# A two-layer trunk kernel: two of four weight sums of a pair made by adding transfers, unsplit weights in a ring of blocks

## The chip, the cores and the metric
The kernel runs on one core of one Trainium2 chip. The metric is the device time of one launch, in microseconds (us), as the median of several runs. A core has five engines with queues of their own, each in order: TensorE (PE, matmuls), VectorE (DVE), ScalarE (ACT), GpSimd (POOL) and SyncE (SP, which here issues most of the DMAs). They wait for each other and for DMAs by semaphores.

## What is computed
Sixteen learned tokens are put ahead of 512 (528 positions, width 1024), which then go through four sub-layers, each followed by a LayerNorm of `alpha * x + f(x)`: a chunked gated DeltaNet (GDN), a gated ConvFFN, a short gated convolution, and a second ConvFFN. The change touches how the weights of the last three are brought in and prepared:

```python
def short_conv_mixer(h, w_in, conv_w, w_out):
    b_gate, c_gate, xv = jnp.split(h @ w_in, 3, axis=-1)
    u = causal_dwconv(c_gate * xv, conv_w)
    return (b_gate * u) @ w_out

def conv_ffn(h, w_up, conv_w, w_down):
    u, gate = jnp.split(h @ w_up, 2, axis=-1)
    u = causal_dwconv(u, conv_w)
    return (jax.nn.silu(u) * gate) @ w_down
```

All of it is float32. D_FF is 2816 (22 blocks of 128), the depthwise convolutions are three wide.

## The kernel before
Channels lie on the 128 partitions and positions run along the rows. `h` holds the activations; `hh` and `hl` are their high and low parts. A weight strip (128 output channels by up to 1024 inputs, so up to 8 blocks of 128 by 128) is loaded as float32 (`raw`), and `split` makes `wh` (ACT, L88) and `wl` (DVE, L89) of it. A block product takes three matmuls: high by high (L272), high by low (L273), low by high (L274).

**Pairs.** Most up-projections of the FFNs, and most input projections of the short conv, are done two strips at a time (18 pairs in each FFN, 8 in the short conv, 44 in all). Each strip is cut into two halves of four blocks, the positions into two halves as well, and the two by two product is done with seven half products rather than eight. Their weights are A11, A12, A22 and four sums: S1 = A21 + A22, S2 = S1 + A11, S3 = A21 + A11, S4 = S2 + A12. Each sum is one DVE add over 128x512 (L210, L212, L214, L216), and each of the seven is then split. `PREP` gives the order in which that is done.

**Staging.** A list of jobs (a pair, or one strip) holds all weights in order of use. `pump` loads the next job as soon as its raw tiles are free and prepares the next piece as soon as the ring of split weights (`wh`, `wl`: 32 blocks, and 24 more once the second part is open) has room; `get` and `product` call it each time a weight is used, so the loads and splits fall between the engine's other instructions at fixed places in the program. Unsplit weights stand in tiles of 8 blocks: two while GDN runs (first part), four afterwards; a pair takes two. The sum tile `s` has 4 blocks.

**Stages of a sub-layer.** An FFN works through its 22 blocks in groups of 4, 6, 6 and 6. The first group is the lead: its up-projections are not paired, since the sums of the activations for the pairs (`sums_a`, `sums_b`, L883) are made in the meantime. `emit` writes the convolution and silu; `gated` multiplies in the gate (L851) and splits the result into `gh`, `gl`; `down` multiplies by the down weights (`pd`) and adds to `h` (L760 for the first group, L762 after). The other groups run as `pairs`, each followed by its `down`. The short conv has a lead of two blocks (`bu0`, `bu1`), then eight pairs. The first pair's weights are loaded and split while the lead still runs, so pair work and lead work share the queues of DVE and ACT there. That is the place of the terms in the prediction.

Of the kernel before, what the change touches and what calls it, by code (L numbers as in the profile page):

```python
# [30 lines left out]
CH = 106  # L31
# [3 lines left out]
LEVELS = (1, 2, 4, 8, 16, 32, 64)  # L35
# [18 lines left out]
NCST = 3 * P  # L54
# [5 lines left out]
PREP = ("A11", "S1", "S2", "A12", "S3", "A22", "S4")  # L60


class Unit:
    def __init__(self, seg, pos, n, hi, lo):
        self.seg, self.pos, self.n, self.hi, self.lo = seg, pos, n, hi, lo


class Job:
    def __init__(self, srcs, nk):
        self.srcs, self.nk, self.raws, self.units, self.ready, self.n = srcs, nk, [], {}, False, 0  # L70


@with_exitstack
def tile_hybrid_trunk(ctx, tc, xt, par, cst, msk, w_ba, w_qkv, w_z, w_ao, w_bi, w_bo, w_up, w_dn, out):
    nc = tc.nc
    V, S, G, TE = nc.vector, nc.scalar, nc.gpsimd, nc.tensor

    cpool = ctx.enter_context(tc.tile_pool(name="cpool", bufs=1))
    hpool = ctx.enter_context(tc.tile_pool(name="hpool", bufs=1))
    wpool = ctx.enter_context(tc.tile_pool(name="wpool", bufs=1))  # L80
    lnp = ctx.enter_context(tc.tile_pool(name="lnp", bufs=1))

    h = hpool.tile([P, KD, T], F32, name="h")
    hh = hpool.tile([P, KD, T], F32R, name="hh")
# [2 lines left out]
    def split(hi, lo, src):  # L87
        S.activation(hi, src, AF.Copy)  # L88
        V.tensor_tensor(lo, src, hi.bitcast(F32), ALU.subtract)  # L89
# [5 lines left out]
    cst_sb = cpool.tile([P, NCST], F32, name="cst_sb")
    msk_sb = cpool.tile([P, len(LEVELS), CH], U8, name="msk_sb")
# [12 lines left out]
    jobs = []  # L109
# [32 lines left out]
    n_gdn = len(jobs) - 8  # L142
# [12 lines left out]
    add_ffn(1)  # L155


    SEG = (32, 24)
    segs = []
    pools = []  # L160
    HOLD6, HOLD8 = 7, 5
    FFN_GRP, SC_GRP = (4, 2), (4, 2)
    STAG = 2
    OUTS = {1: 0, 3: 2, 5: 4, 6: 6, 7: 7}

    def open_part(pool):
        x = len(segs)
        segs.append((pool.tile([P, SEG[x], P], F32R, name=f"wh{x}"), pool.tile([P, SEG[x], P], F32R, name=f"wl{x}")))
        pools.append(pool)

    open_part(wpool)
    state = {"use": 0, "load": 0, "prep": 0, "raws": 0, "base": 0, "held": 0, "seg": 0, "pos": 0, "pairs": 0}
    live = []

    def room(n):

        g_, p_ = state["seg"], state["pos"]
        if p_ + n > SEG[g_]:
            g_, p_ = (g_ + 1) % len(segs), 0
        for u in live:  # L180
            if u.seg == g_ and u.pos < p_ + n and p_ < u.pos + u.n:
                return None
        state["seg"], state["pos"] = g_, p_ + n
        u = Unit(g_, p_, n, segs[g_][0][:, p_ : p_ + n, :], segs[g_][1][:, p_ : p_ + n, :])
        live.append(u)
        return u

    def done(u):
        live.remove(u)

    def load(job):
        for i, src in enumerate(job.srcs):
            x = (state["raws"] - state["base"]) % (2 * len(pools)) // 2
            x = 1 - x if len(pools) == 2 else x
            nm = f"raw{state['raws']}"
# [4 lines left out]
            job.raws.append(raw)  # L200
            state["raws"] += 1
        state["held"] += len(job.srcs)

    def sums(job, what):

        a, b = job.raws
        a11, a12, a21, a22 = a[:, 0:4, :], a[:, 4:8, :], b[:, 0:4, :], b[:, 4:8, :]
        if what == "S1":
            job.s = pools[-1].tile([P, 4, P], F32, name=f"s{job.n}", tag="s", bufs=1)
            V.tensor_tensor(job.s, a21, a22, ALU.add)  # L210
        elif what == "S2":
            V.tensor_tensor(job.s, job.s, a11, ALU.add)  # L212
        elif what == "S3":
            V.tensor_tensor(a21, a21, a11, ALU.add)  # L214
        elif what == "S4":
            V.tensor_tensor(job.s, job.s, a12, ALU.add)  # L216
        own = {"A11": a11, "A12": a12, "A22": a22, "S3": a21}
        return own[what] if what in own else job.s

    def prep_step(job):  # L220

        pair = len(job.srcs) == 2
        what = PREP[len(job.units)] if pair else "all"
        u = room(4 if pair else job.nk)
        if u is None:
            return False
        job.units[what] = u
        if pair:
            split(u.hi, u.lo, sums(job, what))
        else:  # L230
            step = job.nk if job.n else 4
            for k in range(0, job.nk, step):
                split(u.hi[:, k : k + step, :], u.lo[:, k : k + step, :], job.raws[0][:, k : k + step, :])
        job.ready = len(job.units) == (len(PREP) if pair else 1)
        return True

    def pump(end=None):
        while True:
            i = state["load"]
            if i < len(jobs) and i < (n_gdn + 4 if len(pools) == 1 else len(jobs)) \  # L240
                    and state["held"] + len(jobs[i].srcs) <= 2 * len(pools):
                jobs[i].n = i
                load(jobs[i])
                state["load"] += 1
                continue
            i = state["prep"]
            if i >= state["load"] or (end is not None and i >= end):
                return
            if not prep_step(jobs[i]):
                return  # L250
            if jobs[i].ready:
                state["prep"] += 1
                state["held"] -= len(jobs[i].srcs)
# [12 lines left out]

    def mm_steps(ps, u, nk, xh, xl, k0, c0, n, start=True, stop=True, every=2, **kw):
        hi, lo = (u.hi, u.lo) if isinstance(u, Unit) else u
        for k in range(nk):
            r_h = xh[:, k0 + k, c0 : c0 + n]  # L270
            r_l = xl[:, k0 + k, c0 : c0 + n]
            TE.matmul(ps, hi[:, k, :], r_h, start=start and k == 0, stop=False, **kw)  # L272
            TE.matmul(ps, hi[:, k, :], r_l, start=False, stop=False, **kw)  # L273
            TE.matmul(ps, lo[:, k, :], r_h, start=False, stop=stop and k == nk - 1, **kw)  # L274
# [398 lines left out]
    state["base"] = state["raws"]  # L673
# [446 lines left out]
```

## Time and profile before
| what | us |
|---|---|
| median of 3 runs | 1340.49 |
| lowest, highest | 1340.34, 1340.72 |
| time of the profiled execution | 1339.88 |
| its span in the profile | 1338.1 |
| first LayerNorm begins (after GDN) | 413.0 |
| second begins (after the first FFN) | 771.4 |
| third begins (after the short conv) | 954.2 |
| last matmul of the last LayerNorm's means | 1324.2 |

The span runs from the first to the last instruction; the time of an execution adds what lies around it (1.8 us here). In the profile a line such as L89 is the line of the kernel; groups carry the busy time, the mean of one instruction, and the idle time of the engine ahead of it with what ended it. The granted clock of PE is a share of full speed; over the whole span it was 0.996.

### The profile page before, as it was taken

What the parts mean: (1) busy time and instruction counts of PE and PEld (TensorE: products, weight loads), DVE (VectorE), ACT (ScalarE), POOL (GpSimd) and SP (SyncE); (2) the same over time, 40 slices, a digit from 0 to 9 for tenths busy, and PEclk for the clock granted to TensorE, in tenths of its full rate; (3) what the DMA queues carried; (4) which work ended last, traced back from release to release, by engine and by line L of the source; (5) the groups of instructions that cost most, each with busy time, mean ns of one, the idle gap of its engine ahead of it and who ended that gap; (6) DMA issues with size and microseconds to landing.
All of it is one profiled execution on the core that took longest, in us unless ns stands there. A gap on an engine that the chain in (4) does not pass through costs nothing.

```text
span 1338.1 us, 26463 instructions
## 1 busy us (share of the span) xinstructions
PE 1297.5 (97%) x10673; PEld 1251.8 (94%) x10673; DVE 1059.5 (79%) x1934; ACT 766.2 (57%) x1621; POOL 92.0 (7%) x132
## 2 busy tenths in 40 slices
PE   7999999999999999999999999899999999999996
PEld 6899989999899999999999999899998998998996
DVE  6667676776567998969869789899699896886976
ACT  5676767776454646636537465466365573663644
POOL 0322333311110000000000000000000000000000
PEclk9999999999999999999999999899999999999999
DMA  5211111111161142522522412324124342242221
GB/s 199 64 48 33 49 48 35 46 48 33 48 222 45 43 150 67 155 64 87 151 64 84 138 56 79 104 95 150 41 64 126 95 142 79 78 144 72 82 70 64
DMA packets 38395, 115.85 MB, mean 87 GB/s; under 512 B 4224, under 2 KB 7808, under 8 KB 38272
## 3 DMA queue, kind: packets, MB, share of 16 engines
q1 hardware_dynamic: 37632, 112.04, 27.1%
q0 software_dynamic: 640, 2.12, 0.5%
q8 instruction: 83, 1.36, 0.4%
q14 instruction: 40, 0.33, 0.1%
HBM read 112.05 MB, written 2.10 MB: 85 GB/s over the span
## 4 chain that ended last, share of the span: by engine, by line
PE 74%; DVE 16%; ACT 4%; issue 2%; DMA 2%; POOL 2%; SPq 0%; ACTq 0%; POOLq 0%; DVEq 0%
PE pd L273 8%; PE pd L274 8%; PE pd L272 8%; PE px L272 6%; PE px L274 6%; PE px L273 6%; DVE wl L89 3%; PE pz L272 3%; PE pz L273 3%; PE pz L274 3%; PE ps L274 2%; PE ps L273 2%; PE ps L272 2%; PE pq L272 1%; PE pq L274 1%
## 5 line engine op out<-in xcount | busy, mean ns | idle before, releaser
L88 ACT ACTIVATE wh<-raw 128x512 fp32r<-128x512 f32 (+3 forms) x321 | 238.3, 746 | 199.5 <-PE pd L273 82.5
L89 DVE TENSOR_TENSOR wl<-raw,wh 128x512 fp32r<-128x512 f32 (+3 forms) x321 | 264.9, 835 | 63.4 <-ACT wh L88 62.8
L272 PE MATMUL pd<-gh,wh 128*128 128x256 f32 (+3 forms) x704 | 213.2, 306 | 4.8 <-DVE bu L851 3.9
L273 PE MATMUL pd<-gl,wh 128*128 128x256 f32 (+3 forms) x704 | 214.3, 305 | 1.1 <-DVE gl L89 1.0
L274 PE MATMUL pd<-gh,wl 128*128 128x256 f32 (+3 forms) x704 | 213.3, 303 | 0.0
L272 PEld LDWEIGHTS pd<-gh,wh 128*128 128x128 f32 x704 | 132.6, 190 | 11.1 <-DVE bu L851 4.1
L273 PEld LDWEIGHTS pd<-gl,wh 128*128 128x128 f32 x704 | 133.8, 190 | 7.9 <-DVE gl L89 2.1
L274 PEld LDWEIGHTS pd<-gh,wl 128*128 128x128 f32 x704 | 133.7, 190 | 5.8
L88 ACT ACTIVATE wh<-s 128x512 fp32r<-128x512 f32 x132 | 83.2, 630 | 85.0 <-PE pd L273 34.7
L272 PE MATMUL ps<-hh,wh 128*128 128x264 f32 x384 | 114.7, 300 | 0.9 <-ACT acc L411 0.9
L274 PE MATMUL ps<-hh,wl 128*128 128x264 f32 x384 | 115.1, 300 | 0.0
L273 PE MATMUL ps<-hl,wh 128*128 128x264 f32 x384 | 114.3, 298 | 0.0
L273 PE MATMUL pu<-hl,wh 128*128 128x258 f32 (+3 forms) x368 | 105.5, 290 | 0.0
L272 PE MATMUL pu<-hh,wh 128*128 128x258 f32 (+3 forms) x368 | 104.2, 288 | 0.7 <-ACT hh L739 0.7
L274 PE MATMUL pu<-hh,wl 128*128 128x258 f32 (+3 forms) x368 | 104.6, 288 | 0.3 <-DVE wl L89 0.3
L89 DVE TENSOR_TENSOR wl<-s,wh 128x512 fp32r<-128x512 f32 x132 | 90.7, 687 | 15.0 <-ACT wh L88 12.0
L272 PE MATMUL px<-hh,wh 128*128 128x258 f32 (+1 forms) x352 | 99.5, 283 | 0.5 <-ACT sc L933 0.5
L274 PE MATMUL px<-sumh,wl 128*128 128x258 f32 (+1 forms) x352 | 99.7, 283 | 0.0
L273 PE MATMUL px<-suml,wh 128*128 128x258 f32 (+1 forms) x352 | 99.5, 283 | 0.0
L272 PE MATMUL px<-sumh,wh 128*128 128x258 f32 (+1 forms) x352 | 99.4, 282 | 0.0
L274 PE MATMUL px<-hh,wl 128*128 128x258 f32 (+1 forms) x352 | 99.1, 282 | 0.0
L273 PE MATMUL px<-hl,wh 128*128 128x258 f32 (+1 forms) x352 | 99.1, 282 | 0.0
(296 smaller groups left out, 3807.4 us busy)
## 6 DMA issues: line engine op xcount, KB each, us to landing
raw<-in_w_up_dram SPq DMA_DIRECT2D x88, 512.0 KB, 3.8
raw<-in_w_dn_dram SPq DMA_DIRECT2D x48, 384.0 KB, 3.5
raw<-in_w_bi_dram SPq DMA_DIRECT2D x24, 512.0 KB, 4.1
raw<-in_w_qkv_dram SPq DMA_DIRECT2D x23, 512.0 KB, 3.7
raw<-in_w_z_dram SPq DMA_DIRECT2D x8, 512.0 KB, 3.7
raw<-in_w_ao_dram SPq DMA_DIRECT2D x8, 512.0 KB, 3.6
raw<-in_w_dn_dram SPq DMA_DIRECT2D x16, 256.0 KB, 2.7
raw<-in_w_bo_dram SPq DMA_DIRECT2D x8, 384.0 KB, 3.7
```

Of the source, the lines that this page charges most:

```text
L88: S.activation(hi, src, AF.Copy)
L89: V.tensor_tensor(lo, src, hi.bitcast(F32), ALU.subtract)
L272: TE.matmul(ps, hi[:, k, :], r_h, start=start and k == 0, stop=False, **kw)
L273: TE.matmul(ps, hi[:, k, :], r_l, start=False, stop=False, **kw)
L274: TE.matmul(ps, lo[:, k, :], r_h, start=False, stop=stop and k == nk - 1, **kw)
```

## The change
A pair's weights are no longer loaded as two strips of 8 blocks. Five pieces of 4 blocks (256 KB) are loaded by SP, in the order `LOAD`: A21 as the base of S1, A21 again as the base of S3, A11, A12, A22. POOL then issues an accumulating DMA onto each of the first two: A22 onto S1, A11 onto S3. S2 and S4 stay DVE adds (now L241, written onto S1's place). So a pair reads 28 blocks from HBM where it read 16.

Unsplit weights now stand in a ring of blocks, 16 in the first part and 24 more in the second; each piece takes the next free place, and the places of a job are given back when the whole job has been split. `pump` loads piece by piece. To make room, the constants and masks that only GDN uses move to a pool that is given back after it. At three starts of a down stage the high by high matmuls of all streams come ahead of their low parts.

```diff
+LOAD = ("S1", "S3", "A11", "A12", "A22")
...
+class Ring:
+    def room(self, n):
+        g_, p_ = self.at
+        if p_ + n > self.sizes[g_]:
+            g_, p_ = (g_ + 1) % len(self.parts), 0
+        if any(u.seg == g_ and u.pos < p_ + n and p_ < u.pos + u.n for u in self.live):
+            return None
...
-    SEG = (32, 24)
+    WSEG, RSEG = (32, 24), (16, 24)
+    wring, rring = Ring(WSEG), Ring(RSEG)
...
-            raw = pools[x].tile([P, KD, P], F32, name=nm, tag="raw", bufs=2)
-            step = job.nk if state["raws"] else 4
-            for k in range(0, job.nk, step):
-                nc.sync.dma_start(raw[:, k : k + step, :], src[:, k : k + step, :])
...
-        if what == "S1":
-            job.s = pools[-1].tile([P, 4, P], F32, name=f"s{job.n}", tag="s", bufs=1)
-            V.tensor_tensor(job.s, a21, a22, ALU.add)
-        elif what == "S2":
-            V.tensor_tensor(job.s, job.s, a11, ALU.add)
-        elif what == "S3":
-            V.tensor_tensor(a21, a21, a11, ALU.add)
-        elif what == "S4":
-            V.tensor_tensor(job.s, job.s, a12, ALU.add)
...
+    def load_step(job):
+        pair = len(job.srcs) == 2
+        what = LOAD[len(job.raws)] if pair else "all"
+        u = rring.room(4 if pair else job.nk)
+        if u is None:
+            return False
+        raw = u.aps[0]
+        job.raws[what] = u
+        if pair:
+            a, b = job.srcs
+            part = {"A11": a[:, 0:4], "A12": a[:, 4:8], "A21": b[:, 0:4], "A22": b[:, 4:8]}
+            first, *more = {"S1": ("A21", "A22"), "S3": ("A21", "A11")}.get(what, (what,))
+            nc.sync.dma_start(raw, part[first])
+            for x in more:
+                nc.gpsimd.dma_start(raw, part[x], accum_op=ALU.add)
...
+            raw = job.raws["S1" if what in ("S2", "S4") else what].aps[0]
+            more = {"S2": "A11", "S4": "A12"}.get(what)
+            if more:
+                V.tensor_tensor(raw, raw, job.raws[more].aps[0], ALU.add)
+            split(hi, lo, raw)
...
+        if job.ready:
+            for r in job.raws.values():
+                rring.done(r)
```

Rows of an engine's queue follow, in program order. A row has the line, the operation, what it writes and reads (a number in a name only tells tiles apart; `raw0`, `raw1` are the two parts of the ring), its shape, and the semaphores it waits for: DMAHW for DMAs of SP, DMASW for those of POOL, and the engines.

DVE in the lead of the short conv, before. `raw132` and `raw133` are the two strips of the first pair, `raw134` is the second pair's; `bu1` is the second block of the lead:

```order
L851 TENSOR_TENSOR bu1_10218<-bu1_10218,pu106_7_0_10397 128x258 [waits PE_49]
L89 TENSOR_TENSOR hl_69<-sc_5027,hh_68 128x2x258 [waits Activation_49]
L89 TENSOR_TENSOR wl0_83<-raw132_10306,wh0_82 128x512 [waits DMAHW2_49,Activation_49]
L89 TENSOR_TENSOR wl0_83<-raw132_10306,wh0_82 128x512 [waits Activation_49]
L210 TENSOR_TENSOR s114_10320<-raw133_10308 128x512 [waits DMAHW3_49]
L89 TENSOR_TENSOR wl0_83<-raw133_10308,wh0_82 128x512 [waits Activation_49]
L214 TENSOR_TENSOR raw133_10308<-raw133_10308,raw132_10306 128x512 [waits DVE_49]
L89 TENSOR_TENSOR wl0_83<-s114_10320,wh0_82 128x512 [waits Activation_49]
L89 TENSOR_TENSOR wl1_5016<-raw134_10314,wh1_5015 128x512 [waits DMAHW4_49,Activation_49]
L212 TENSOR_TENSOR s114_10320<-s114_10320,raw132_10306 128x512 [waits DVE_49]
L89 TENSOR_TENSOR wl0_83<-raw133_10308,wh0_82 128x512 [waits Activation_49]
L851 TENSOR_TENSOR bu1_10218<-bu1_10218,pu106_7_1_10422 128x256 [waits PE_49]
```

DVE at that place now; `raw1_4982` holds A21's sums for the first pair, then the second pair's pieces:

```order
L241 TENSOR_TENSOR raw1_4982<-raw1_4982,raw0_87 128x512 [waits DVE_49]
L119 TENSOR_TENSOR wl0_86<-raw1_4982,wh0_85 128x512 [waits DMASW5_49]
L119 TENSOR_TENSOR wl0_86<-raw0_87,wh0_85 128x512 [waits DMAHW4_49,Activation_49]
L119 TENSOR_TENSOR wl0_86<-raw1_4982,wh0_85 128x512 [waits Activation_49]
L861 TENSOR_TENSOR bu0_10122<-bu0_10122,pu105_6_0_10243 128x258 [waits PE_49]
L861 TENSOR_TENSOR bu0_10122<-bu0_10122,pu105_6_1_10268 128x256 [waits PE_49]
L241 TENSOR_TENSOR raw1_4982<-raw1_4982,raw0_87 128x512 [waits DVE_49]
L119 TENSOR_TENSOR wl1_4981<-raw1_4982,wh1_4980 128x512 [waits DMAHW7_49]
L119 TENSOR_TENSOR gl_4990<-bu0_10122,gh_4989 128x514 [waits Activation_49]
L119 TENSOR_TENSOR wl1_4981<-raw1_4982,wh1_4980 128x512 [waits Activation_49]
L861 TENSOR_TENSOR bu1_10140<-bu1_10140,pu106_7_0_10309 128x258 [waits PE_49]
L861 TENSOR_TENSOR bu1_10140<-bu1_10140,pu106_7_1_10334 128x256 [waits PE_49]
```

Before, both gates of `bu0` came ahead of the pair and the second gate of `bu1` stood behind seven steps of it. Now the first pair's work down to S2's split stands ahead of both gates of `bu0`, and S4's add with splits between them and the two gates of `bu1`; L210 and L214 are gone.

ACT at that place now (`bc2` is the start of a third block's product, `gh` the high part of a gated block, `hh` that of an activation sum):

```order
L1022 ACTIVATE bc2_10001<-pu104_4_1_10144 128x258 [waits PE_49]
L118 ACTIVATE wh0_85<-raw0_87 128x512 [waits DMAHW4_49,PE_49]
L118 ACTIVATE wh1_4980<-raw1_4982 128x512 [waits DMAHW7_49,PE_49,Activation_49]
L118 ACTIVATE wh0_85<-raw1_4982 128x512 [waits DVE_49]
L118 ACTIVATE wh1_4980<-raw0_87 128x512 [waits DMASW6_49,PE_49,Activation_49]
L118 ACTIVATE gh_4989<-bu0_10122 128x514 [waits DVE_49]
L118 ACTIVATE wh1_4980<-raw1_4982 128x512 [waits DVE_49]
L118 ACTIVATE gh_4989<-bu1_10140 128x514 [waits DVE_49]
```

Row by row: `gh` of `bu0` stands behind a split that waits for POOL's DMA of the second pair (DMASW6). Before, `gh` of `bu0` was issued ahead of the pair's splits and `gh` of `bu1` behind four of them.

DVE in the lead of the first FFN, before (`c1_2` and `c1_3` are the last two blocks of the lead, `raw52` to `raw55` strips of down weights, `raw56` and `raw57` the first pair):

```order
L89 TENSOR_TENSOR wl1_5016<-raw53_6037,wh1_5015 128x512 [waits DMAHW3_49,Activation_49]
L851 TENSOR_TENSOR c1_2_5952<-c1_2_5952,pu47_6_1_6094 128x258 [waits PE_49]
L89 TENSOR_TENSOR wl1_5016<-raw54_6041,wh1_5015 128x512 [waits DMAHW4_49,Activation_49]
L851 TENSOR_TENSOR c1_3_5964<-c1_3_5964,pu48_7_0_6128 128x258 [waits PE_49]
L89 TENSOR_TENSOR gl_5024<-c1_2_5952,gh_5023 128x516 [waits Activation_49]
L89 TENSOR_TENSOR wl1_5016<-raw55_6045,wh1_5015 128x512 [waits DMAHW5_49,Activation_49]
L851 TENSOR_TENSOR c1_3_5964<-c1_3_5964,pu48_7_1_6153 128x258 [waits PE_49]
L883 SCALAR_TENSOR_TENSOR sc_5027<-sc_5027,h_67 128x520
L89 TENSOR_TENSOR wl1_5016<-raw56_6051,wh1_5015 128x512 [waits DMAHW6_49,Activation_49]
L89 TENSOR_TENSOR wl0_83<-raw56_6051,wh0_82 128x512 [waits Activation_49]
L210 TENSOR_TENSOR s56_6065<-raw57_6053 128x512 [waits DMAHW7_49]
L89 TENSOR_TENSOR gl_5024<-c1_3_5964,gh_5023 128x516 [waits Activation_49]
```

DVE there now:

```order
L119 TENSOR_TENSOR wl1_4981<-raw1_4982,wh1_4980 128x512 [waits DMAHW4_49]
L119 TENSOR_TENSOR wl1_4981<-raw1_4982,wh1_4980 128x512 [waits DMAHW5_49]
L119 TENSOR_TENSOR wl1_4981<-raw1_4982,wh1_4980 128x512 [waits DMAHW6_49]
L119 TENSOR_TENSOR wl1_4981<-raw1_4982,wh1_4980 128x512 [waits DMASW0_49,Activation_49]
L861 TENSOR_TENSOR c1_2_5908<-c1_2_5908,pu47_6_0_6019 128x258 [waits PE_49]
L861 TENSOR_TENSOR c1_2_5908<-c1_2_5908,pu47_6_1_6044 128x258 [waits PE_49]
L241 TENSOR_TENSOR raw1_4982<-raw1_4982 128x512 [waits DVE_49]
L119 TENSOR_TENSOR wl0_86<-raw1_4982,wh0_85 128x512 [waits DMAHW1_49,Activation_49]
L119 TENSOR_TENSOR gl_4990<-c1_2_5908,gh_4989 128x516 [waits Activation_49]
L119 TENSOR_TENSOR wl0_86<-raw1_4982,wh0_85 128x512 [waits Activation_49]
L861 TENSOR_TENSOR c1_3_5920<-c1_3_5920,pu48_7_0_6078 128x258 [waits PE_49]
L861 TENSOR_TENSOR c1_3_5920<-c1_3_5920,pu48_7_1_6103 128x258 [waits PE_49]
```

The split of S1, which waits for POOL's DMA (DMASW0), and S2's add and split have moved ahead of the gates of `c1_3`; before, two splits and the add of S1 stood between those gates and `gl`.

More of the change, by code (lines that the diff above doesn't have):

```diff
@@ L60, with __init__, done @@
 PREP = ("A11", "S1", "S2", "A12", "S3", "A22", "S4")
+LOAD = ("S1", "S3", "A11", "A12", "A22")
 class Unit:
-    def __init__(self, seg, pos, n, hi, lo):
-        self.seg, self.pos, self.n, self.hi, self.lo = seg, pos, n, hi, lo
+    def __init__(self, seg, pos, n, aps):
+        self.seg, self.pos, self.n, self.aps = seg, pos, n, aps
+class Ring:
+    def __init__(self, sizes):
+        self.sizes, self.parts, self.live, self.at = sizes, [], [], (0, 0)
+    def room(self, n):
[4 more added lines that the diff above has]
+            return None
+        self.at = g_, p_ + n
+        u = Unit(g_, p_, n, [t_[:, p_ : p_ + n, :] for t_ in self.parts[g_]])
+        self.live.append(u)
+        return u
+    def done(self, u):
+        self.live.remove(u)
 class Job:
     def __init__(self, srcs, nk):
-        self.srcs, self.nk, self.raws, self.units, self.ready, self.n = srcs, nk, [], {}, False, 0
+        self.srcs, self.nk, self.n = srcs, nk, 0
+        self.raws, self.units, self.loaded, self.ready = {}, {}, False, False
 @with_exitstack
@@ L81, in tile_hybrid_trunk @@
     lnp = ctx.enter_context(tc.tile_pool(name="lnp", bufs=1))
+    gctx = ExitStack()
+    gp = gctx.enter_context(tc.tile_pool(name="gp", bufs=1))
     h = hpool.tile([P, KD, T], F32, name="h")
@@ L94, in tile_hybrid_trunk @@
     par_sb = cpool.tile([P, NPAR], F32, name="par_sb")
[L95 to L96 removed]
+    cst_sb = gp.tile([P, NCST], F32, name="cst_sb")
+    msk_sb = gp.tile([P, len(LEVELS), CH], U8, name="msk_sb")
     ba_raw = lnp.tile([P, KD, 16], F32, name="ba_raw", tag="c", bufs=CB)
@@ L166, in open_part @@
     def open_part(pool):
-        x = len(segs)
-        segs.append((pool.tile([P, SEG[x], P], F32R, name=f"wh{x}"), pool.tile([P, SEG[x], P], F32R, name=f"wl{x}")))
-        pools.append(pool)
+        x = len(rring.parts)
+        wring.parts.append((pool.tile([P, WSEG[x], P], F32R, name=f"wh{x}"), pool.tile([P, WSEG[x], P], F32R, name=f"wl{x}")))
+        rring.parts.append((pool.tile([P, RSEG[x], P], F32, name=f"raw{x}"),))
     open_part(wpool)
-    state = {"use": 0, "load": 0, "prep": 0, "raws": 0, "base": 0, "held": 0, "seg": 0, "pos": 0, "pairs": 0}
@@ L173, in tile_hybrid_trunk @@
[L173 to L195, printed above, removed]
-            raw = pools[x].tile([P, KD, P], F32, name=nm, tag="raw", bufs=2)
-            step = job.nk if state["raws"] else 4
-            for k in range(0, job.nk, step):
-                nc.sync.dma_start(raw[:, k : k + step, :], src[:, k : k + step, :])
-            job.raws.append(raw)
-            state["raws"] += 1
-        state["held"] += len(job.srcs)
@@ L204, in sums @@
-    def sums(job, what):
-        a, b = job.raws
-        a11, a12, a21, a22 = a[:, 0:4, :], a[:, 4:8, :], b[:, 0:4, :], b[:, 4:8, :]
-        if what == "S1":
-            job.s = pools[-1].tile([P, 4, P], F32, name=f"s{job.n}", tag="s", bufs=1)
-            V.tensor_tensor(job.s, a21, a22, ALU.add)
-        elif what == "S2":
-            V.tensor_tensor(job.s, job.s, a11, ALU.add)
-        elif what == "S3":
-            V.tensor_tensor(a21, a21, a11, ALU.add)
-        elif what == "S4":
-            V.tensor_tensor(job.s, job.s, a12, ALU.add)
-        own = {"A11": a11, "A12": a12, "A22": a22, "S3": a21}
-        return own[what] if what in own else job.s
+    state = {"use": 0, "load": 0, "prep": 0, "pairs": 0}
@@ new lines, in tile_hybrid_trunk @@
+    done = wring.done
+    def load_step(job):
[13 more added lines that the diff above has]
+                nc.gpsimd.dma_start(raw, part[x], accum_op=ALU.add)
+        else:
+            step = job.nk if job.n else 4
+            for k in range(0, job.nk, step):
+                nc.sync.dma_start(raw[:, k : k + step, :], job.srcs[0][:, k : k + step, :])
+        job.loaded = len(job.raws) == (len(LOAD) if pair else 1)
+        return True
@@ L223, in prep_step @@
         what = PREP[len(job.units)] if pair else "all"
-        u = room(4 if pair else job.nk)
+        u = wring.room(4 if pair else job.nk)
         if u is None:
@@ L227, in prep_step @@
         job.units[what] = u
+        hi, lo = u.aps
         if pair:
-            split(u.hi, u.lo, sums(job, what))
+            raw = job.raws["S1" if what in ("S2", "S4") else what].aps[0]
[3 more added lines that the diff above has]
+            split(hi, lo, raw)
         else:
+            raw = job.raws["all"].aps[0]
             step = job.nk if job.n else 4
             for k in range(0, job.nk, step):
-                split(u.hi[:, k : k + step, :], u.lo[:, k : k + step, :], job.raws[0][:, k : k + step, :])
+                split(hi[:, k : k + step, :], lo[:, k : k + step, :], raw[:, k : k + step, :])
         job.ready = len(job.units) == (len(PREP) if pair else 1)
+        if job.ready:
+            for r in job.raws.values():
+                rring.done(r)
         return True
@@ L239, in pump @@
             i = state["load"]
-            if i < len(jobs) and i < (n_gdn + 4 if len(pools) == 1 else len(jobs)) \
-                    and state["held"] + len(jobs[i].srcs) <= 2 * len(pools):
+            if i < len(jobs) and (len(rring.parts) == 2 or i < n_gdn + 4):
                 jobs[i].n = i
-                load(jobs[i])
-                state["load"] += 1
-                continue
+                if load_step(jobs[i]):
+                    state["load"] += jobs[i].loaded
+                    continue
             i = state["prep"]
-            if i >= state["load"] or (end is not None and i >= end):
+            if i >= state["load"] or (end is not None and i >= end) or not prep_step(jobs[i]):
                 return
[L249 to L253, printed above, removed]
+            state["prep"] += jobs[i].ready
     def get():
@@ L267, in mm_steps @@
     def mm_steps(ps, u, nk, xh, xl, k0, c0, n, start=True, stop=True, every=2, **kw):
-        hi, lo = (u.hi, u.lo) if isinstance(u, Unit) else u
+        hi, lo = u.aps if isinstance(u, Unit) else u
         for k in range(nk):
@@ L292, in tile_hybrid_trunk @@
     strict = cst_sb[:CH, C_STR : C_STR + CH]
-    strict_r = cpool.tile([P, CH], F32R, name="strict_r")
+    strict_r = gp.tile([P, CH], F32R, name="strict_r")
     V.tensor_copy(strict_r[:CH], strict)
-    one1 = cpool.tile([P, P], F32, name="one1")
+    one1 = gp.tile([P, P], F32, name="one1")
     V.memset(one1, 1.0)
@@ L310, in bcm @@
         return ap.unsqueeze(1).to_broadcast([ap.shape[0], n, ap.shape[1]])
-    with ExitStack() as gctx:
-        gp = gctx.enter_context(tc.tile_pool(name="gp", bufs=1))
+    with gctx:
         pm = gctx.enter_context(tc.tile_pool(name="pm", bufs=2, space=PSUM))
```

5 lines of the change are left out of this document (1 added, 4 removed).

## The prediction
> **What bounds the kernel now.** I read the busy shares first, then stage windows, then the waits of the matmul engine (PE), then the timeline of the places where it waited. Page, its first part and the chain that ended last:
> ```profile
> span 1338.1 us, 26463 instructions
> PE 1297.5 (97%) x10673; PEld 1251.8 (94%) x10673; DVE 1059.5 (79%) x1934; ACT 766.2 (57%) x1621; POOL 92.0 (7%) x132
> ...
> PE 74%; DVE 16%; ACT 4%; issue 2%; DMA 2%; POOL 2%; SPq 0%; ACTq 0%; POOLq 0%; DVEq 0%
> ```
> PE is busy 97% of the span. A share is an average, so here are windows over the pair stages (columns: window, length, busy us of each engine, granted clock, DMA share, GB/s):
> ```profile
> 500.00:680.00 180.00, 179.51 (x1494) 178.92 (x1493) 147.09 (x252) 96.59 (x179) 0.00 (x0) 1.00 0.34 102
> 680.00:800.00 120.00, 119.99 (x996) 119.51 (x995) 99.40 (x192) 66.61 (x125) 0.00 (x0) 1.00 0.30 90
> 870.00:960.00 90.00, 90.00 (x749) 89.71 (x748) 76.57 (x140) 46.62 (x89) 0.00 (x0) 1.00 0.31 100
> 1030.00:1150.00 120.00, 120.00 (x830) 111.72 (x829) 97.30 (x160) 63.32 (x115) 0.00 (x0) 1.00 0.34 102
> 1240.00:1320.00 80.00, 80.00 (x670) 79.77 (x669) 67.23 (x131) 43.50 (x83) 0.00 (x0) 1.00 0.21 63
> 870.00:900.00 30.00, 30.00 (x253) 30.00 (x252) 29.66 (x53) 18.42 (x37) 0.00 (x0) 1.00 0.25 83
> ```
> In the pair stages PE has no gap to give back, at full clock, with as many matmuls as before the change and after it. The last row is the strongest: VectorE (DVE) is busy 29.66 of 30 us there and PE still 30.00. So the adds that the change removes are hidden. What PE waited for from 440 us on, where the changed order begins:
> ```profile
> PE pd L272 <- DVE bu L851: 3.9, 1, 3.9
> PE pd L273 <- DVE gl L89: 1.0, 2, 0.6
> PE pd L272 <- DVE h L760: 0.9, 1, 0.9
> PE pu L272 <- ACT hh L739: 0.7, 1, 0.7
> PE px L272 <- ACT sc L933: 0.5, 1, 0.5
> ```
> These five sum to 7.0 us: nearly all that better feeding could win. The large one, in the lead stage of the short conv:
> ```profile
> 836.03 0.28 PE L274 MATMUL pd<-gh,wl 128*128 128x258 f32 x1
> 840.20 0.58 PE L272 MATMUL pd<-gh,wh 128*128 128x256 f32 x1 [3.88 <-DVE bu L851]
> 830.00:835.00 5.00, 5.00 (x44) 5.00 (x44) 3.83 (x9) 3.28 (x7) 0.00 (x0) 1.00 0.91 287
> 835.00:840.00 5.00, 1.32 (x12) 1.11 (x10) 5.00 (x9) 3.22 (x6) 0.00 (x0) 0.89 0.39 147
> 840.00:845.00 5.00, 4.70 (x20) 4.41 (x21) 4.80 (x10) 1.68 (x3) 0.00 (x0) 0.50 0.65 193
> 845.00:850.00 5.00, 5.00 (x38) 4.80 (x38) 4.37 (x11) 1.37 (x3) 0.00 (x0) 0.93 0.06 21
> ```
> After the 3.88 us gap the granted clock is 0.50 for five us: 20 matmul records there against 44 before the gap. The half-clock stretch costs about 5 x (1 - 0.50) = 2.5 us, less 0.3 of waiting inside it: about 2.
>
> The Trainium skill, "TensorE: Matmul & The Clock Gate", says that an idle PE loses its clock; the trace agrees, 0.50 behind 3.88 us.
>
> **The change part by part.** *Two adds fewer for each of 44 pairs.*
> ```profile
> L210 DVE TENSOR_TENSOR s<-raw 128x512 f32<-128x512 f32 x44 | 30.3, 688 | 0.7
> L214 DVE TENSOR_TENSOR raw<-raw,raw 128x512 f32<-128x512 f32 x44 | 30.2, 686 | 0.4
> ```
> L210 and L214 go: 30.3 + 30.2 = 60.5 us of DVE, 1.37 us a pair. By the windows this is worth 0 to PE in the steady part, where matmuls hide it. It counts only where DVE is what PE waits for, at the leads.
>
> *88 accumulating DMAs.* The trace holds none. The nearest rows: the strip loads that SP issues, and the eight transfers of x that POOL issues.
> ```profile
> raw<-in_w_up_dram SPq DMA_DIRECT2D x88, 512.0 KB, 3.8
> raw<-in_w_dn_dram SPq DMA_DIRECT2D x16, 256.0 KB, 2.7
> h<-in_xt_dram POOLq DMA_DIRECT2D x8, 259.0 KB, 6.3
> L668 POOL DMA_DIRECT2D h<-in_xt_dram x8: 548/548/768, 378.5 to 383.4; - x8
> DMA to landing us min/median/max: 3.1/6.3/8.4
> 378.00:380.00 2.00, 1.41 (x12) 1.20 (x12) 2.00 (x5) 2.00 (x5) 1.49 (x3) 1.00 0.38 144
> ```
> Call X the time of an accumulate from issue to landing. POOL's transfers of nearly the same size took 3.1 to 8.4 us, median 6.3; but they were issued within 5 us of each other and lay in flight together. In a pair stage there are two for each 10.2 us, so I take X = 4, nearest to the 3.1 of one that had the engines to itself, plus some for reading twice. The ends, 3.1 and 8.4, go into the range, and beyond 8.4 is a rival, because an addition may be slower than any row here. Issuing is 0.55 us on an idle POOL; DVE was busy 2.00 of 2.00 us in the last row while POOL issued three, so a busy DVE did not stop it.
>
> The Trainium skill, "SBUF — State Buffer", "Who interferes with whom", has a rule against the change: a copy or tensor_scalar in DVE's two-port mode locks GpSimd out, and so its descriptor writing, for the instruction; a tensor_tensor does not. The row above agrees with the second half; no run here shows the first. By it some accumulates would start up to one L842 (0.48 us) late, and the sum would be 0 to 1.5 us higher over three leads.
> ```profile
> L842 DVE TENSOR_SCALAR c<-u,par_sb 128x516 f32<-128x516 f32 (+1 forms) x8 | 3.7, 481 | 0.0
> ```
>
> *More bytes.* A pair read 8 + 8 blocks, 1.0 MB; now 5 x 256 KB from SP and 2 x 256 KB from POOL, 1.75 MB. The DMA share in pair stages goes from 0.34 to 0.34 x 1.75 = 0.60, or 0.34 x 2.25 = 0.77 if an accumulate costs twice. Below 1, so not a bound. SP's five issues replace two, 3 x 0.33 us more a pair on a queue that does nothing else.
>
> *The steady ring.* Two pairs of 20 blocks fill the 40. Pair k+2 is loaded when the last split of pair k is done.
> ```profile
> 517.55 0.69 DVE L210 TENSOR_TENSOR s<-raw 128x512 f32<-128x512 f32 x1
> 523.98 0.69 DVE L216 TENSOR_TENSOR s<-s,raw 128x512 f32<-128x512 f32 x1
> 527.78 0.68 DVE L210 TENSOR_TENSOR s<-raw 128x512 f32<-128x512 f32 x1
> ```
> A pair takes 10.2 us. The last split of a pair ends some 1.3 us behind the add at 523.98, at 525.3; the first sum of the pair after the next is wanted at 527.8 + 10.2 = 538.0, or 1.2 us earlier if DVE runs ahead. That leaves 11.5 us for 0.3 of waiting, the 2.7 of a 256 KB load, and X. With X = 4 it is 7.0: hidden. It shows from X = 8.5 on.
>
> *The short conv's lead.* Here DVE did pair work before the gate that PE waited for.
> ```profile
> 839.73 0.42 DVE L851 TENSOR_TENSOR bu<-bu,pu 128x256 f32<-128x256 f32 x1
> 841.87 0.69 DVE L89 TENSOR_TENSOR gl<-bu,gh 128x514 fp32r<-128x514 f32 x1
> ```
> From 835.48 to 839.73 DVE ran seven steps of the first pair (three adds and four splits, a new one each 0.60 us) and then the gate. The order rows above show what stands there now: the first pair's splits ahead of both gates of bu0, and only two splits and one add between those and the gates of bu1. Stepping through both engines with 0.60 a DVE step and 0.63 an ACT split, with the pair's accumulates landed: bu0's split on ACT ends at 836.5 to 837.2 (so PE now starts its down products late by about 2 us), bu1's gate near 838.9, its gl ends near 840.8 instead of ending at 841.87 + 0.69 = 842.56, when PE takes it; the difference is -1.75. If the single gap of 3.88 becomes two shorter ones, the half clock may not come, whose part behind 842.6 is 2.7 us at 0.50, another -1.35 (the part ahead of it lay under the wait for gl). The cover here is thin: the first pair's S1 is split ahead of bu0, so from X of about 5 each us of X delays this place by one.
>
> *The FFN leads.*
> ```profile
> 478.36 0.69 DVE L89 TENSOR_TENSOR gl<-c,gh 128x516 fp32r<-128x516 f32 x1
> 479.10 0.39 PE L273 MATMUL pd<-gl,wh 128*128 128x260 f32 x1 [0.58 <-DVE gl L89]
> 484.90 0.39 PE L272 MATMUL pd<-gh,wh 128*128 128x260 f32 x1 [0.89 <-DVE h L760]
> 1021.87 0.50 PE L273 MATMUL pd<-gl,wh 128*128 128x512 f32 x1 [0.46 <-DVE gl L89]
> ```
> In the first FFN S1's split, S2's add and S2's split come ahead of the gate of c1_3, so its gl ends near 480.1, not 479.05: +1.05; DVE is then through with pair work and the 0.89 wait goes: +0.2 together. In the second FFN, where the other of the two waits for gl stands, the same step through the order delays its last gl from 1021.9 to 1022.6 and there is no later wait to win back: +0.7. Both assume X below 4 to 6.
>
> *Down stages.* Three 6-block strips of the down weights now fit at once instead of two, so the 0.5 us wait for sc (ACT was held by a strip's DMA) may go: -0.5, worst 0. The GDN part's order on DVE and ACT is the same; masks and constants change their pool only; the k order at the down starts (hi products of all streams first) moves waits by less than 0.1. All 0.
>
> Sum at X = 4: 0 - 1.75 + 0.2 + 0.7 - 0.5 = -1.35, with 0.35 of the clock's 1.35 added as a middle: **-1.7**. Against the profiled execution, 1339.88 (span 1338.1): 1338.2. The median shown is 0.6 above that execution, so **1338.8**.
>
> **Rivals.** (A) *Late accumulates at the leads*: slower. ACT and DVE run in order; a split that waits for an accumulated sum holds the silu, gates and gl splits queued behind it, and PE waits for those. It decides at X of 5: every us beyond costs about 1 at each of three leads. X = 6.3 gives -1.7 + 3 x 1.3 = +2.2 (1342.7), X = 8.4 gives +8.5 (1349). For: POOL's median of 6.3. Against: that was eight at once.
>
> (B) *Late accumulates in every pair*, X above 8.5: each pair then waits about half the excess, since two are in flight. X = 12 gives 1.75 x some 40 pairs = +70 (1410). Against: no row is that long.
>
> (C) *The leads close wholly*: the short conv's gap and half clock go (3.9 + 2) with part of the FFN waits: -4 to -7, 1333.5 to 1336.5. For: DVE has 1.37 us less per pair exactly where PE waits for DVE, and loads come earlier. Against: the order puts bu0's gate later.
>
> (D) *It does nothing*: adds hidden, order neutral: DVE 60 us less busy, time 1339.7 to 1341.5.
>
> The Trainium skill, "Collectives: The Full Stack", "The bandwidth ceiling: the fold count and why AG ≠ RS ≠ AR", says that an adding transfer is slower for its two source reads. No run so far shows it. With the fit in "DMA: Bandwidth & Descriptors", "Anatomy of one DMA — SWDGE (gpsimd) path", 2.0 us + bytes / 436 GB/s, my estimate is 2.6 us plain and 3.2 read twice; the sum would stay at -1.7.
>
> **How the numbers follow.** Forecast 0.44 (0.12 of it beyond -2.7), A 0.18 (0.14 beyond +2.7), B 0.10, C 0.20, D 0.08. About 0.2%, 2.7 us, is what a measurement of this kernel can tell from no change. Faster: 0.12 + 0.20 = 0.32; slower: 0.14 + 0.10 = 0.24; same: 0.44. The range leaves out B, the last of C below -6 and A above +7.5: 1334.5 to 1348. The forecast's own range is -3.5 to 0: 1337 to 1340.5.
>
> **What would show it.** DVE about 60 us less busy, no gain of PE in the pair windows; POOL rows with 88 issues and X beside them (4 by me; 6 for A; above 8.5 for B). In the short conv's lead two gaps in place of one, the larger under 3 us, and the clock above 0.9 behind it. In the FFN leads a wait of about 1.5 us for gl of c1_3 and none for h L760. I am wrong if pair windows show PE below 99% waiting for a sum's split, if X is above 5, or if bu0's gate now comes later than 837.

## The result, and the profile after
The changed kernel takes 1383.97 us (median of 4 runs, 1380.92 to 1386.46) against 1340.41 before: a ratio of 1.0322, 95% interval [1.0309, 1.0334]. It is 43.6 us slower, where 1338.8 had been forecast and 1348 was the end of the range.

The page of the changed kernel, busy times and the chain that ended last:

```profile
span 1384.7 us, 26946 instructions
PE 1317.1 (95%) x10673; PEld 1265.9 (91%) x10673; DVE 1009.7 (73%) x1846; ACT 760.4 (55%) x1621; POOL 168.5 (12%) x220
...
PE 62%; DVE 14%; DMA 12%; ACT 5%; issue 4%; POOL 2%; SPq 0%; ACTq 0%; POOLq 0%; DVEq 0%
```

DVE is 50 us less busy, about what the two adds a pair should give (a new instruction starts each 0.60 us in a series, and 88 x 0.60 = 53). What is new is DMA with 12% of the chain where it had 2%. The windows of the pair stages (the same columns as in the prediction) now have holes in PE:

```profile
500.00:680.00 180.00, 171.31 (x1372) 169.67 (x1371) 128.34 (x216) 93.87 (x174) 18.22 (x21) 0.96 0.57 144
880.00:980.00 100.00, 94.83 (x764) 93.83 (x763) 69.85 (x121) 44.85 (x88) 6.92 (x8) 0.97 0.51 138
1070.00:1190.00 120.00, 115.38 (x798) 108.32 (x798) 84.00 (x138) 61.12 (x115) 12.17 (x14) 0.97 0.59 142
```

PE was 179.51 of 180 us busy in the first window before and is 171.31 now, and its clock is 0.96. What PE waits for over the whole span (us in total, times, longest):

```profile
PE px L284 <- ACT sc L935: 22.2, 11, 3.9
...
PE px L284 <- ACT sc L943: 6.4, 6, 2.2
PE pd L284 <- ACT gh L118: 3.1, 3, 2.4
...
PE px L284 <- ACT sc L929: 1.2, 3, 0.4
```

L929, L935 and L943 are small copies of a product out of PE's accumulators on ACT; they take 0.37 us. They are late because of what stands ahead of them in ACT's queue. ACT and PE in one stall of the first FFN's pairs, from the timeline:

```profile
521.44 0.37 ACT L935 ACTIVATE sc<-px 128x260 f32<-128x260 f32 x1
526.08 1.15 ACT L118 ACTIVATE wh<-raw 128x512 fp32r<-128x512 f32 x2 [4.26 <-DMA raw<-in_w_up_dram]
...
537.54 0.63 ACT L118 ACTIVATE wh<-raw 128x512 fp32r<-128x512 f32 x1 [5.07 <-DMA raw<-in_w_up_dram]
538.08 0.71 ACT L850 ACTIVATE c<-pu,ntap 128x516 f32<-128x516 f32 x1
538.70 0.36 ACT L935 ACTIVATE sc<-px 128x260 f32<-128x260 f32 x1
```

```profile
539.11 0.59 PE L284 MATMUL px<-sumh,wh 128*128 128x260 f32 x1 [3.32 <-ACT sc L935]
```

ACT stands for 4.26 and then 5.07 us at a weight split whose data has not landed, and PE then waits 3.32 us for the copy behind the second one. The chain of waits around the first shows what that data had to go through:

```profile
516.02 0.61 DVE wl L119
516.65 3.63 DMA raw<-in_w_up_dram
520.33 0.49 issue
520.82 5.24 DMA raw<-in_w_up_dram
526.08 0.64 ACT wh L118
```

This is one S1. Its place in the ring comes free when DVE has read the last sum of the pair before the previous one (516.63); SP loads A21 (3.63 us), POOL issues the accumulating DMA (0.49 later), that takes 5.24, and ACT starts 20 ns after it has landed. From load to landing it is 9.4 us; call this the chain. ACT was ready at 521.81, 5.2 us after the place came free; call this the room. POOL's DMAs over the run, with how they were waited for:

```profile
L219 POOL DMA_DIRECT2D raw<-in_w_up_dram x72: 856/865/1174, 467.8 to 1303.3; - x72
...
who waited for it (us, times):
  ACT wh L118: 83.4, 25
...
DMA to landing us min/median/max: 3.7/5.0/8.7
```

ACT waited 83.4 us for accumulates, in 25 places. Followed load by load through the trace, these are all sums S1 but for one: 24 of the 44 S1 splits start within 0.2 us of the landing, while the accumulates of S3 land 7.5 us or more before their splits start in all pairs but five near the start of a group (median 12.2). The 24 had 2.7 to 8.2 us of room; the chain of an S1 has a median of 8.5.

Then the clock. In the window behind the 3.32 us wait it is at half:

```profile
540.00:545.00 5.00, 5.00 (x25) 5.00 (x25) 5.00 (x11) 3.50 (x7) 0.00 (x0) 0.50 0.40 111
```

The mean clock is 0.984 (0.996 before): 1384.7 x 0.016 = 22.2 us of clock lost against 1338.1 x 0.004 = 5.4, so 16.8 more. PE's waits from 440 us on sum to 34.0 (the four rows above, 0.7 and 0.4) where five rows had 7.0 before: 27.0 more. Together 43.8 of the 46.6 us by which the span grew. This is the profiled execution, the slowest of the four; in the other three the mean clock was 0.988 to 0.990, by the same sum 8 to 11 us of clock, so that share varies from execution to execution.

### The profile page after: what moved, and what is told of

It is laid out like the page before. It is cut to its first block, busy times and chain, and to the rows that moved or that the text cites. A ratio compares the mean times of both kernels' runs of the same rounds, so it can differ in the third digit from the quotient of the medians.

```text
span 1384.7 us, 26946 instructions
## 1 busy us (share of the span) xinstructions
PE 1317.1 (95%) x10673; PEld 1265.9 (91%) x10673; DVE 1009.7 (73%) x1846; ACT 760.4 (55%) x1621; POOL 168.5 (12%) x220
## 4 chain that ended last, share of the span: by engine, by line
PE 62%; DVE 14%; DMA 12%; ACT 5%; issue 4%; POOL 2%; SPq 0%; ACTq 0%; POOLq 0%; DVEq 0%
DMA raw<-in_w_up_dram 9%; PE pd L285 8%; PE pd L286 8%; PE pd L284 8%; DVE wl L119 4%; PE px L284 4%; PE px L285 3%; PE px L286 3%; DMA raw<-in_w_bi_dram 3%; PE ps L286 2%; PE ps L285 2%; PE ps L284 2%; ACT wh L118 2%; PE pz L284 2%; PE pz L285 1%
## 5 line engine op out<-in xcount | busy, mean ns | idle before, releaser
L118 ACT ACTIVATE wh<-raw 128x512 fp32r<-128x512 f32 (+3 forms) x453 | 316.4, 712 | 350.7 <-PE pd L285 131.3
L119 DVE TENSOR_TENSOR wl<-raw,wh 128x512 fp32r<-128x512 f32 (+3 forms) x453 | 354.2, 794 | 168.4 <-ACT wh L118 163.6
L219 POOL DMA_DIRECT2D raw<-in_w_up_dram x72 | 62.6, 893 | 664.8 <-DMA raw<-in_w_up_dram 453.3
L284 PE MATMUL px<-sumh,wh 128*128 128x258 f32 (+1 forms) x352 | 105.2, 299 | 23.4 <-ACT sc L935 22.2
L284 PE MATMUL px<-hh,wh 128*128 128x258 f32 (+1 forms) x352 | 102.3, 291 | 6.4 <-ACT sc L943 6.4
L286 PE MATMUL px<-sumh,wl 128*128 128x258 f32 (+1 forms) x352 | 103.3, 294 | 0.0
L285 PE MATMUL px<-suml,wh 128*128 128x258 f32 (+1 forms) x352 | 103.1, 293 | 0.0
L284 PEld LDWEIGHTS px<-sumh,wh 128*128 128x128 f32 x352 | 70.0, 199 | 27.1 <-ACT sc L935 24.8
```

Source lines behind the costliest of these rows:

```text
L219: nc.gpsimd.dma_start(raw, part[x], accum_op=ALU.add)
```

## The experiments
Each ratio is to the kernel before, on the same chip, with its 95% interval.

**One sum at a time.** Three kernels give back the DVE add of S1, of S3, or of both, in the ring as it is; the edit of the first:

```diff
-            first, *more = {"S1": ("A21", "A22"), "S3": ("A21", "A11")}.get(what, (what,))
+            first, *more = {"S1": ("A21",), "S3": ("A21", "A11")}.get(what, (what,))
...
-            more = {"S2": "A11", "S4": "A12"}.get(what)
+            more = {"S1": "A22", "S2": "A11", "S4": "A12"}.get(what)
```

> S1 is again a DVE add (A22 onto A21 in the ring, 0.69 us x 44); S3 keeps its accumulating DMA. Theory T (S1's place is held by S2 and S4 until the pair's last split, and load 2.8 + hop 0.5 + accumulate 5 us then take longer than the some 5 us until S1's split is due; S3 has 12 us to spare): the waits of ACT for S1 go, 1337 to 1342 us, about the time of before. Rival traffic (the 75% more bytes and the read-modify-writes slow all loads): half the extra POOL transfers are left, 1355 to 1370. Rival order (the ring and the scheduler's new order of splits stall PE whoever adds): stays at 1380 or more.

> S3 is again a DVE add (A11 onto A21 in the ring); S1 keeps its accumulating DMA. Theory T: S1's chain is as long as in the change, 1375 to 1390 us. Rival traffic: half the extra POOL transfers are left, 1355 to 1370. Rival order: 1380 or more.

> No accumulating DMA: five loads of four blocks a pair into the ring, all four sums on DVE. Theory T: 1336 to 1341 us, the ring's own small gain at the leads left over. Rival traffic: 1340 to 1350 (1.25 MB a pair instead of 1.75). Rival order: 1380 or more.

S1 on DVE: 1352.22, ratio 1.0096 [1.0072, 1.0119]. S3 on DVE: 1383.93, 1.0332 [1.0308, 1.0356]. Both: 1345.16, 1.0035 [1.0022, 1.0049]. In the second, ACT's waits for POOL's DMAs:

```profile
  ACT wh L118: 79.7, 22
```

Half of the accumulates are gone there, the time has not moved and the wait hardly (83.4 before): the price hangs on S1, and the rival of traffic falls. The rival that the ring and the new order stall PE whoever adds falls with the third, 1345.16; that the order has a part all the same is shown below. In the first and the third no instruction waits for POOL's landings any more. They did not come all the way back, though: 12 and 5 us were left where none were expected. In the first, PE waits at the starts of down stages for something else:

```profile
PE pd L285 <- DVE gl L119: 6.9, 6, 3.1
```

The two longest of these, 3.1 and 2.4 us, lie behind sums on DVE that wait for a plain load of SP, and DVE does so in 22 places, where it did in none before the change:

```profile
569.82 0.69 DVE L241 TENSOR_TENSOR raw<-raw 128x512 f32<-128x512 f32 x1 [3.00 <-DMA raw<-in_w_up_dram]
```

```profile
DVE raw L241 <- DMA raw<-in_w_up_dram: 33.8, 22, 4.9
```

So part of the wait has moved from ACT to DVE. Both kernels make S1 from a piece (A22) that is loaded last, which fits; that these sums are S1 is not shown. PE's waits from 440 us on, 14.9 us against 9.3 before, are 5.6 of the first kernel's 11 us of longer span; the rest is open.

**S1's place freed early.** S2 is written onto A11's place and S4 too; places are given back one by one:

```diff
-            raw = job.raws["S1" if what in ("S2", "S4") else what].aps[0]
-            more = {"S2": "A11", "S4": "A12"}.get(what)
+            raw = job.raws["A11" if what in ("S2", "S4") else what].aps[0]
+            more = {"S2": "S1", "S4": "A12"}.get(what)
...
+            for x in {"S2": ("S1",), "S3": ("S3",), "A22": ("A22",), "S4": ("A11", "A12")}.get(what, ()):
+                rring.done(job.raws[x])
```

> Both accumulating DMAs stay; S2 and S4 are written onto A11's place instead of S1's, and each place is given back when it has been read last, so S1's place is free after S2's add and not after S4's split, some 5 us sooner a pair. Theory T: room grows from about 5 to about 10 us against a chain of 8.3 to 9.4, so most of the stall goes: 1338 to 1350 us. Rival traffic and rival order: the same bytes and nearly the same order, 1375 to 1390.

1346.89, ratio 1.0043 [1.0028, 1.0058]: 37 of the 43.6 us are back, with every byte and both accumulates in place. ACT's waits for POOL, and one of its waits that is left:

```profile
  ACT wh L118: 10.4, 4
```

```profile
885.13 1.67 ACT L118 ACTIVATE wh<-raw 128x512 fp32r<-128x512 f32 x3 [3.97 <-DMA raw<-in_w_bi_dram]
```

That wait is for A11, whose place now stays occupied to the end, and whose plain load took 5.5 us (issued at 879.64) beside an accumulate in flight. By this row the stall had moved on to the piece that now inherits the late place, with a shorter chain and a smaller price.

**A plain copy, and no second transfer.** The first keeps the whole change with POOL copying instead of adding, so it leaves out the additions of S1 and S3; the second drops S1's second transfer, so it leaves out the addition of S1. The edit of the first:

```diff
-                nc.gpsimd.dma_start(raw, part[x], accum_op=ALU.add)
+                nc.gpsimd.dma_start(raw, part[x])
```

> POOL's 88 DMAs copy instead of adding (the additions of S1 and S3 are left out; every place, wait and order stays as in the change). Two serial transfers remain. If the addition costs little beside the second transfer (theory T with a chain of two transfers): POOL's median from issue to landing falls from 5.0 to about 4.4 us and the time to 1370 to 1382. If the addition itself is the price (rival: reading the destination back doubles the transfer): about 3.0 us and 1345 to 1360.

> The change without the second transfer of S1 (the addition of A22 onto S1 is left out; S3 still accumulates; places, the times at which they come free and the order of use as in the change). S1's chain is one load, 2.8 us, below the room of about 5. Theory T: 1337 to 1344 us. With the change at 1384 (5.0 us more in the chain) and plain copies at 1356 (3.5 us more) that is the third point of time against chain. Rival traffic: 1355 to 1370, since S3's transfers remain.

1355.93, ratio 1.0116 [1.0102, 1.0129], and 1337.76, ratio 0.9980 [0.9971, 0.9989]. POOL's copies in the first:

```profile
L219 POOL DMA_DIRECT2D raw<-in_w_up_dram x72: 546/546/548, 467.7 to 1272.9; - x72
...
who waited for it (us, times):
  ACT wh L118: 45.6, 17
...
DMA to landing us min/median/max: 2.8/3.5/5.3
```

The addition costs 1.5 us more in flight than a copy (5.0 against 3.5), more than theory T gave it (0.6) and less than the rival (2.0). The time lies in the range of the rival, 1345 to 1360, and below the 1370 of theory T: the addition itself is a large part of the price. Taken as a line through the two times: 28.0 us of time for 1.5 us, 18.7 for each us of the second transfer; on it nothing is left to lose below about 2.5 us (3.5 less (1355.93 - 1337.76) / 18.7). That is an estimate; no run has a second transfer between 0 and 3.5 us. With no second transfer nothing is lost, and the time is below the one before.

**All places freed early.** S4's sum is made right behind A12's split, onto A12's place, so places come free in the order S1, A11, S3, A22, A12 and are filled in that order; in the second kernel S1 is a DVE add again, in the third S3 as well:

```diff
+LOAD = ("S1", "A11", "S3", "A22", "A12")
...
+            raw = at({"S2": "A11", "S4": "A12"}.get(what, what))
+            if what == "S2":
+                V.tensor_tensor(raw, raw, at("S1"), ALU.add)
+            split(hi, lo, raw)
+            if what == "A12":
+                V.tensor_tensor(raw, raw, at("A11"), ALU.add)
```

> Both accumulating DMAs stay. As in the run that freed S1's place early, but S4's sum is made right behind A12's split onto A12's place, so the places come free in the order S1, A11, S3, A22, A12, and the pieces are loaded in that order. Theory T (a place must come free early enough for its chain): S1 keeps 5 us or more to spare, A11's load (which waited up to 4 us when S2 and S4 stood on its place) gets some 4 us more; ACT's waits for DMA in the pair stages go, 1335 to 1341 us. Rival traffic: 1345 or more, as when S1's place alone was freed.

> As the run before it, but S1 is a DVE add of A22 onto A21; S3 alone accumulates. Theory T: S1's split no longer waits for a chain of two transfers but for A22's place, which comes free at the sixth of seven splits: 1336 to 1342. Rival traffic: half the extra POOL transfers, 3 to 6 us below the run before it.

> Ring, places freed early, no accumulating DMA: five loads a pair, all four sums on DVE as before the change. If adding transfers are worth something at the leads where DVE is waited for: 1341 to 1344, slower than the runs with places freed early and one or two accumulates (1340.2 and 1341.0). If their gain and cost are both hidden: the same within 2 us, 1338 to 1342.

1341.02, 1.0003 [0.9994, 1.0012]; 1340.19, 0.9994 [0.9985, 1.0003]; 1341.33, 1.0010 [1.0001, 1.0019]. With two, one or no accumulating transfer a pair the time is that of before within 0.2%. The differences among the three are too small to tell whether adding transfers are worth anything at the leads. Nothing of the some 50 us of adds that DVE is spared, and nothing of the 34.6 MB (44 pairs by 12 blocks of 64 KB) that are read in addition, shows beyond 0.2% once places come free in time.

**The order alone.** One thing separates the two programs in the pair stages that the diff does not tell. Before, S1, S2 and S4 of all pairs shared one tile `s`, so the next pair's S1 could not be made before S4 had been split. With its own place, S1 can be split first, and the scheduler (the part of the build that orders each engine's queue) did that. ACT's queue at one pair of the first FFN, before (`s58` is one pair's tile, `s59` the next one's, rows left out between):

```
L88 ACTIVATE wh0_82<-s58_6476 128x512 [waits PE_49]
...
L88 ACTIVATE wh0_82<-s59_6631 128x512 [waits DVE_49]
```

and in the changed kernel (`raw0` is the next pair's S1, with its wait for POOL's DMA; the last row is S4 of the pair before):

```
L118 ACTIVATE wh0_85<-raw0_87 128x512 [waits DMASW7_49,PE_49]
...
L118 ACTIVATE wh0_85<-raw1_4982 128x512 [waits PE_49]
```

In time, before (S4, the next S1, the S1 after that) and now (S1 first, then S4):

```profile
515.20 0.63 ACT L88 ACTIVATE wh<-s 128x512 fp32r<-128x512 f32 x1 [0.28 <-PE pz L273]
518.27 0.63 ACT L88 ACTIVATE wh<-s 128x512 fp32r<-128x512 f32 x1 [0.41 <-DVE s L210]
...
528.50 0.63 ACT L88 ACTIVATE wh<-s 128x512 fp32r<-128x512 f32 x1
```

```profile
508.38 0.63 ACT L118 ACTIVATE wh<-raw 128x512 fp32r<-128x512 f32 x1 [0.50 <-PE pz L285]
...
514.12 0.63 ACT L118 ACTIVATE wh<-raw 128x512 fp32r<-128x512 f32 x1
```

Now the S1 after that is wanted one pair later than the S1 that ran ahead, and so only some 8 us behind S4 (514.12 to 521.81) rather than 13 (515.20 to 528.50). The next kernel is the change with both transfers and all places as they are; S1's split only takes a zero that the split of S4 of the pair before wrote:

```diff
-            split(hi, lo, raw)
+            if what == "S1":
+                S.activation(hi, raw, AF.Identity, bias=tok)
+                V.tensor_tensor(lo, raw, hi.bitcast(F32), ALU.subtract)
+            else:
+                split(hi, lo, raw)
+            if what == "S4":
+                S.activation(tok, hi[:, 0, 0:1].bitcast(F32), AF.Copy, scale=0.0)
```

> The change, with one thing added: a pair's S1 split on ACT takes a zero that the split of S4 of the pair before has written (44 more ACT instructions of 128x1), so S1 can no longer be split ahead of that S4, as it could not before the change, when both stood in one tile. Places, transfers and bytes are the change's. Theory T2 (the room for S1's chain was short because the schedule moved S1's split of the next pair some 8 us ahead of S4's, so the one after it was wanted some 5 us behind S4's): room is back at about 8 to 9 us against a chain of 8.3 to 9.4, 1340 to 1352 us. Theory T without the order (any S1 that waits for the place S4 leaves is late): 1375 to 1390.

1338.28, ratio 0.9987 [0.9978, 0.9997]: 45.7 us below the change, and slightly below the kernel before. ACT at two pairs' border, from the timeline:

```profile
523.13 0.63 ACT L118 ACTIVATE wh<-raw 128x512 fp32r<-128x512 f32 x1 [0.28 <-PE pz L293]
523.80 0.20 ACT L250 ACTIVATE tok<-wh 128x1 f32<-128x1 f32 x1
524.03 0.72 ACT L245 ACTIVATE wh<-raw,tok 128x512 fp32r<-128x512 f32 x1
```

S4, the zero, S1, with no wait for DMA. Who waits for POOL's transfers there, and their durations:

```profile
  ACT wh L245: 7.1, 4
  ACT wh L118: 1.8, 1
...
DMA to landing us min/median/max: 3.6/4.8/7.9
```

```profile
500.00:680.00 180.00, 178.26 (x1482) 177.58 (x1481) 133.79 (x227) 99.29 (x188) 19.87 (x23) 1.00 0.58 151
870.00:960.00 90.00, 90.00 (x747) 89.59 (x746) 71.28 (x133) 46.80 (x90) 5.67 (x7) 1.00 0.48 135
```

The transfers are as long as in the change (4.8 against 5.0) and just as many; the wait for them fell from 83.4 to 8.9 us (7.1 of it for S1, of which 5.2 at the very first pair, where the ring has just been opened), and PE is 99 to 100% busy in the windows again. S1's median chain is 8.5 us, as in the change; the room is about 9 us in the steady pairs, and the six that still started at the landing had 7.0 to 9.0, but for that first one.

**Both remedies.** Places freed early, and the order held:

> Both remedies together: places freed early (S1 0.8 us to several us to spare became 5 and more) and S1's split held behind S4's of the pair before. If either alone takes the stall away (theory T2: the room only has to exceed the chain), the second adds nothing: 1336 to 1341 us, within 0.2% of the run with the held order alone (1338.3) and of the one with places freed early (1341.0). If the slack left in those runs still cost time: below 1336.

1338.86, ratio 0.9991 [0.9982, 1.0000]. Neither remedy adds anything clear to the other.

## Why the prediction was wrong
- **Right:** the adds were hidden. PE is not faster by one of the 50 us that DVE saved, and with every stall gone the three kernels with two, one and no accumulating transfer agree within 0.1%.
- **Right in kind, near in size partly by luck:** the leads. In the short conv's lead PE's large wait went from 3.9 us to the first row below, and in the first FFN's lead two waits of 0.9 and 0.6 us to the second:

```profile
PE pd L284 <- ACT gh L118: 2.4, 1, 2.4
```

```profile
PE pd L284 <- ACT gh L118: 0.3, 1, 0.3
```

  The short conv's -1.5 stands near the -1.75 predicted, and bu0's split is what PE waits for, as predicted. But there is one gap and not two, the granted clock behind it was 0.74 (860 to 865 us) where above 0.9 had been named, and `gh` of bu0 was late because it stood on ACT behind a split that waited for an accumulate:

```profile
850.43 6.56 DMA raw<-in_w_bi_dram
```

```profile
857.09 0.63 ACT L118 ACTIVATE wh<-raw 128x512 fp32r<-128x512 f32 x1 [3.30 <-DMA raw<-in_w_bi_dram]
```

  That is the mechanism of rival A at this lead. The first FFN gave -1.2 where +0.2 had been worked out, the second 0.0 (0.8 us of waits before and after) where +0.7 had. The kernel with the order held, 1338.28, lies where the sum had put the change; since the terms do not come out one by one, that is no proof of them.
- **Mis-sized:** X. It was taken as 4 and its median is 5.0 (3.7 to 8.7), inside the bounds and below the 8.5 from which the steady pairs were to stall, so in the prediction's sum it changes nothing. By the line of the two transfers' runs the 1.0 us is worth some 19 of the 43.6. The estimates beside the sum, 2.6 for a copy and 3.2 read twice, were both low: 3.5 and 5.0.
- **The step that failed:** "That leaves 11.5 us for 0.3 of waiting, the 2.7 of a 256 KB load, and X." The room was read off the timeline of before, from one pair's last split to the S1 of the pair after the next. Two things made it smaller. The larger: the distance held only while S1 could not overtake S4, which the shared tile enforced and the change took away; the late pairs had 2.7 to 8.2 us. The changed order was looked up for the leads and not for the pairs, where the sum's zero for the steady part rested on it. The smaller: the last split does not end "some 1.3 us behind the add at 523.98, at 525.3". A place comes free when DVE's low part has been read from it, and in the trace of before that is 526.56 + 0.69 = 527.25:

```profile
526.56 0.69 DVE L89 TENSOR_TENSOR wl<-s,wh 128x512 fp32r<-128x512 f32 x1
```

  So even with the order of before it was about 9.5 by the prediction's own working (538.0 - 1.2 - 527.25), and about 9 in the run with the order held. That run shows that the first decides: against a chain of 8.5, 9 is enough, and 5 is not.
- **The rival that came true** is B, late accumulates in every pair, with a chance of 0.10. Its mechanism was right; its point of decision was wrong. It was set at X above 8.5 and, by the estimate from the line of the two transfers' runs, lies near 2.5. Since X was thought to decide alone, the row "no row is that long" spoke against it, and the room was never given bounds of its own.
- **The clock** was counted at one lead only. In the profiled execution of the change it fell to a half in eight stretches, each behind a wait of PE of 2.1 to 3.9 us, seven of them inside the pairs: 16.8 of the 46.6 us by the sum above.

## What to carry to other kernels
A transfer is hidden by room and not by being short: work out when its buffer comes free and when its reader stands first in its queue, both in the order of the changed program, and give that difference bounds as one does for an unknown duration. A shared buffer is also an order: when a change gives each user its own place, the scheduler may run the next user ahead, and what follows that user in an in-order queue then waits for the slowest chain. If a buffer that takes the longest chain to fill is the last to be freed, write the late sums elsewhere, or hold the order; here a dependency that costs ACT 0.2 us a pair gave back 45.7 us.

## What the runs showed of the hardware that was not expected
An accumulating DMA of 256 KB took 0.86 us to issue and 5.0 us from issue to landing (medians), the same DMA as a copy 0.55 and 3.5. The queue of POOL's DMAs in the change and in the run with copies (packets, MB, share of 16 engines' span):

```profile
q0 software_dynamic: 13312, 25.20, 11.1%
```

```profile
q0 software_dynamic: 7680, 25.20, 5.9%
```

Without the 640 packets and 0.5% that both kernels share with the one before, that is 144 packets and 0.106 x 1384.7 / 88 = 1.67 us of all sixteen engines for one accumulate, against 80 packets and 0.054 x 1355.4 / 88 = 0.83 us for one copy. The Trainium skill, "Collectives: The Full Stack", "The bandwidth ceiling: the fold count and why AG ≠ RS ≠ AR", gives the second source read as the reason why the ReduceScatter collective, which adds, is half as fast as a copying one. The trace agrees for this kernel's own transfers as far as it goes: the engines' time is twice a copy's, though the bytes counted are the same. No run here shows the reads themselves.
